# A hybrid decoder step on one core: the reciprocal square root of the norms as one GpSimd power

## The chip, the core and the metric

The kernel runs on one core of one Trainium2 chip. The metric is device time in microseconds (us) of the whole launch. A core has five engines with instruction queues of their own, which run in order and wait for each other by semaphores: TensorE (PE, with its weight loads PEld), VectorE (DVE), ScalarE (ACT), GpSimd (POOL) and SyncE (SP), which here issues nearly all DMAs.

## What is computed

The reference is one inference step of a 2-layer decoder, for a prompt of 2048 tokens and 8 samples of 8 tokens, with 1024 features. Each layer modulates its input, projects it (`z = h @ w_in[l]`), and gives pieces of z to four mixers that share the width: A differential attention, B a causal spatial gate, C a convolution module, D a gated linear recurrence (HGRN2). The outputs are gated, concatenated, projected, added to the residual and normalized. All of the norms need one number per row, or per row and head:

```
def _layer_norm(x, g, b):
    xc = xf - xf.mean(-1, keepdims=True)
    var = (xc * xc).mean(-1, keepdims=True)
    return xc * lax.rsqrt(var + EPS) * g + b
def _rms_norm(x, g):
    return xf * lax.rsqrt((xf * xf).mean(-1, keepdims=True) + EPS) * g
```

`_rms_norm` stands behind A and D (per head of 64 columns), `_layer_norm` in B and C (256 columns) and at the end of the layer (1024 columns).

## The kernel before

Tokens lie in tiles of 128 rows, 16 tiles for the prompt and one of 64 rows for the samples. A layer has two phases.

**Projections** (in the trace about 0 to 1040 us for layer 0 and 1640 to 2640 us for layer 1). In two groups of 1024 tokens, slabs of w_in are loaded, split by ACT and POOL into a high and a low part (`wh`, `wl`; the subtraction is `sub_lo`, L172, mostly on POOL), and multiplied on PE in three products into PSUM tiles `z`. The work of B, C and D is woven in: B's gate norm (`b_v`), C's 31 taps on DVE (`c_taps`, L1013) and its norm (`c_norm`), D's chain of blocks (`d_levels`) and its head norm (`d_norm`).

**Attention and output** (about 1040 to 1640 us and 2640 to 3202 us). For each block of query tiles and head, PE makes the scores (L668), DVE takes the row maximum from PSUM (L672), ACT the exponential (L676), DVE combines the two softmaxes (L697, L702), PE transposes (L715), ACT copies (L717), PE multiplies by the values (L720). The end of `attn_value` (from L731 on) sums squares per head, calls rsqrt for `sma` and scales `ot` by the result (L742); POOL applies the gain (L746). One block behind, `out_tile` does the output projection (L1360 to L1362), residual and LayerNorm of a tile; its rsqrt is that of `smo`, used by `nb` (L1372) and by ACT (L1376), after which POOL applies gain and offset (L1377, L1378).

`rsqrt(v, M, n, who, pool)` (L174 to L191) starts from the exponent bits (shift L179 on DVE, subtraction L181) and makes three Newton steps. With `pool` false it runs on DVE alone in 11 instructions (L179, L181, three times L183, L189, L190). With `pool` true, one shift stays on DVE and 13 instructions run on POOL (L181, three times L183, L185, L186, L187). There are 124 calls. The table KN sets who runs where: D (20 calls, up to 8 columns) and the sample's attention (2 calls, 4 columns) on POOL; A (40 calls, 4 or 2 columns), the LayerNorm of the outputs (34 calls, 1 column), B (18 calls, 2 columns or 1) and C (10 calls, 4 columns or 1) on DVE. The names of the columns carry the stream: `smd`, `sms`, `sma`, `smo`, `smb`, `smc`, with `y` for the result, `a` and `i` for the helpers.

The order of each engine's queue is not the order of the code: the tile framework simulates the program with its own durations and priorities and lays every queue out by that simulation. A change of one helper therefore moves instructions on all engines.

Of the kernel before, what the change touches and what calls it, by code (L numbers as in the profile page):

```python
# [9 lines left out]
F32 = mybir.dt.float32  # L10
F32R = mybir.dt.float32r
BF16 = mybir.dt.bfloat16
I32 = mybir.dt.int32
U8 = mybir.dt.uint8
AF = mybir.ActivationFunctionType
ALU = mybir.AluOpType
# [52 lines left out]
def hymba_step_kernel(  # L69
# [21 lines left out]
    # order, engines and buffers: P* offsets of priority, E* / L* / R* choice of engine, the others counts and orders  # L91
# [16 lines left out]
    def cpy(k, out, in_):  # L108
        """copy by ScalarE or VectorE"""
        (nc.vector.tensor_copy if KN[k] else nc.scalar.copy)(out, in_)  # L110
# [18 lines left out]
    # pools of the phase: PSUM banks of the projections, a second bank for transposes  # L129
# [21 lines left out]
    def st(tag, dt=F32):  # L151
        """rows of 512 of the streams that run beside each other: zs slabs, ms branches, os input and output"""
        return stp.tile([P, 512], dt, tag=tag, name=nm(tag), bufs=NST[tag])

    # small columns: width by stream
# [18 lines left out]
    def rsqrt(v, M, n, who, pool=True):  # L174
        """1 / sqrt(v) in place for v [M, n] > 0: estimate from the exponent bits, three Newton steps."""
        i = sm(who, "i", 2)[0:M, 0:n]
        y = sm(who, "y", 2)[0:M, 0:n]
        a = sm(who, "a", 2)[0:M, 0:n]
        nc.vector.tensor_scalar(i, v.bitcast(I32), 1, None, op0=ALU.logical_shift_right)  # L179
        eng = nc.gpsimd if pool else nc.vector  # L180
        eng.tensor_scalar(y.bitcast(I32), i, -1.0, float(0x5F3759DF), op0=ALU.mult, op1=ALU.add)  # L181
        for _ in range(3):
            eng.tensor_tensor(a, v, y, ALU.mult)  # L183
            if pool:
                eng.tensor_tensor(a, a, y, ALU.mult)  # L185
                eng.tensor_scalar(a, a, -0.5, 1.5, op0=ALU.mult, op1=ALU.add)  # L186
                eng.tensor_tensor(y, y, a, ALU.mult)  # L187
            else:
                eng.scalar_tensor_tensor(a, a, -0.5, y, op0=ALU.mult, op1=ALU.mult)  # L189
                eng.scalar_tensor_tensor(y, a, 1.5, y, op0=ALU.add, op1=ALU.mult)  # L190
        return y  # L191

    def gate2(dst, t, x):
        """2 silu(x) = (tanh(x / 2) + 1) x, given t = tanh(x / 2)"""
        nc.vector.scalar_tensor_tensor(dst, t, 1.0, x, op0=ALU.add, op1=ALU.mult)  # L195

# [7 lines left out]
    nc.vector.tensor_copy(identb, ident)  # L204
    cmaskb = cp.tile([P, 128], BF16, name="cmaskb")
# [7 lines left out]
    # page indices: row = (layer * NPOOL + page) * 128 + partition  # L213
# [15 lines left out]
    # conditioning vectors, transposed  # L229
# [50 lines left out]
    def mod(l, Lx, part, mp, bank=None):  # L280
        """shift, 1 + scale or gate of the rows of c, features on partitions."""
        dst = (Lx.shT, Lx.sc1T, Lx.gT)[part]
        for half in range(2):
# [7 lines left out]
            # the four sums are added once features are on partitions  # L291
# [23 lines left out]
    def prep(l, Lx, hp):  # L315
        """small tensors of a layer; hp: those that only the first phase needs"""
# [19 lines left out]
        with tc.tile_pool(name=nm("prep"), reuse_waits="tile", bufs=1) as pp:  # L336
# [16 lines left out]
            # lower bound: cumulative softmax over the layers, without the first  # L353
# [18 lines left out]
            # head norms; A and D carry the 1/2 of their gate  # L372
# [4 lines left out]
            # lambda of the differential attention  # L377
# [11 lines left out]
            # convolution taps  # L389
# [7 lines left out]
            # 1/4: the halves of the swish and of the gate  # L397
# [3 lines left out]
            # spatial weights, lower triangle  # L401
# [10 lines left out]
            # 1/2 of the gate in the weights and in the bias  # L412
# [13 lines left out]
    # state kept between the groups of a layer  # L426
# [92 lines left out]
    def tok_pairs(g):  # L519
        """(first token column, global tile, number of tiles, rows, is sample)"""  # L520
        out = [(i * P, g * GT + i, 2, P, False) for i in range(0, GT, 2)]
        if g == 0:
            out.append((TG, NT, 1, NS, True))
        return out
# [19 lines left out]
    def mix(main, n, *fills):  # L544
        """main (about n steps) with each fill (generator, steps, share of main over which it is spread) in between"""
# [18 lines left out]
    # ================= A: differential attention =================  # L564
# [55 lines left out]
    def attention(l, t0, nt, Lx, ap, act=None):  # L620
        """nt tiles of queries from tile t0"""
# [31 lines left out]
    def attn_probs(qi, qt, kst, l1, Lx, ap):  # L653
        """p1 - lam (l1 / l2) p2, unnormalized; l1"""
# [6 lines left out]
        for m in range(2):  # L661
            pms = []
            for pc, n in enumerate(sizes):
# [7 lines left out]
                # negated running maximum  # L671
# [7 lines left out]
            if npc > 1:  # L679
                # factor of the first part, whose maximum may have been smaller  # L680
# [24 lines left out]
    def attn_value(qi, pm, vst, acc, ls, j4, nt, hd, act, Lx, l, ap):  # L705
        """values of even key tiles on the lower columns of the array, of odd ones on the upper"""
# [21 lines left out]
        # transposed, the two halves of the columns added  # L728
# [11 lines left out]
        ss = rsqrt(ss, P, nt, "a", KN["RA"] and act is None)  # L740
# [8 lines left out]
    def attention_sample(l, Lx, Sx, ap):  # L749
# [91 lines left out]
        ss = rsqrt(ss, NS, 4, "s", KN["RS"])  # L841
# [6 lines left out]
    # ================= gates =================  # L848
# [12 lines left out]
    def gate_pair(l, g, h, ca, cb):  # L861
        """two slabs, by block of tokens: the first block is done with early"""
# [29 lines left out]
    # ================= B: spatial gate =================  # L892
    def b_v(l, g, h, Lx):
        def consume(ps, ti, n, M, smpl):
# [9 lines left out]
            rstd = rsqrt(rstd, M, n, "b", KN["RB"])  # L904
# [32 lines left out]
    # ================= C: convolution =================  # L937
# [81 lines left out]
    def c_norm_(l, g, C, acc, t0, n, smpl, Lx):  # L1019
# [13 lines left out]
            rstd = rsqrt(rstd, M, nt, "c", KN["RC"])  # L1033
# [24 lines left out]
    # ================= D: HGRN2 =================  # L1058
    def d_v(l, g, h, Sx, dp):
        Sx.di = dp.tile([P, GT, 256], F32, name=nm("di"))  # L1060
        if g == 0:
            # the sample rows on both halves of the partitions
# [12 lines left out]
    def d_init(g, Sx, dp):  # L1075
        """buffers of the chain of blocks, late ones first: they take the place of the convolution's"""
# [41 lines left out]
    def d_gate(f, p, n, Lx, Sx):  # L1118
        """f in place, and 1 - f"""
# [6 lines left out]
    def d_levels(q, f, k, n, levels, dp, Sx):  # L1126
        """masked products of all levels for blocks of 64 tokens: source tokens of a pair of blocks on partitions,
        (head, pair, target token) along the row (sample: the two heads on the partition halves); the products of a
        block with the one before it are left in PSUM; leaves prefix and suffix products."""
# [7 lines left out]
        def product(s, col, A, ia, B, ib, hh, par):  # L1137
            # the row tiles of the two heads work at the same time: never in one quadrant of a bank
# [49 lines left out]
    def d_norm(po, M, nq, dst, Lx):  # L1188
        """RMS norm over the 64 value columns of each head; po: [M, nq*64] in PSUM"""
# [5 lines left out]
        ss = rsqrt(ss, M, nq, "d", KN["RD"])  # L1195
# [4 lines left out]
    def d_block(l, g, p, b, q, f, Lx, Sx, dp):  # L1200
        k = d_gate(f, p, 512, Lx, Sx)
        att, sx, E = yield from d_levels(q, f, k, 512, LEVELS + (64,), dp, Sx)
        # source tokens of a pair of blocks x target tokens; the target before the source stays zero
# [78 lines left out]
    # ================= output projection, residual, LayerNorm =================  # L1282
    def out_weights(l, op):
        """w_out in two parts, and the rows of the epilogue"""
# [16 lines left out]
    def out_gate(l, O, smpl):  # L1301
        """gate rows of the sample or of the prompt"""
# [7 lines left out]
    # order of the rows of w_out: A and D (transposed here), B and C (features on partitions already)  # L1310
# [251 lines left out]
```

## Time and profile before

| what | value |
|---|---|
| time, median of 3 runs | 3179.31 us (3175.09 to 3195.48) |
| profiled execution: span | 3202.3 us, 22.99 us above the median of the runs |
| PE, DVE, ACT, POOL busy | 2881.2, 2280.8, 1223.5, 1122.6 us |
| granted TensorE clock, mean | 0.954 |

The span runs from the first to the last instruction of one profiled execution; that execution has no other time of its own in the data, so its span stands for it. A busy time is the time in which the engine had an instruction in work, a wait inside an instruction included. Matmuls overlap, and their ends are modelled.

### The profile page before, as it was taken

How to read it: one execution, taken by the hardware profiler on the slowest of the kernel's cores; microseconds unless marked ns; L12 is line 12 of the kernel's file. 1: busy time of each engine (PE TensorE's matmuls, PEld its weight loads, DVE VectorE, ACT ScalarE, POOL GpSimd, SP SyncE). 2: the span in 40 equal slices, each digit the busy share in tenths (PEclk: the TensorE clock that was granted, in tenths of full speed). 3: DMA queues.
4: the chain of work that ended last, by engine and by line, in shares of the span. 5: the costliest groups of instructions: out<-in, count | busy, mean ns of one | idle time of the engine just before them, and what ended most of it. 6: DMA issues, size and time to landing. Idle time of an engine off the chain costs nothing. (4 is left out here: it accounts for less than half of the span.)

```text
span 3202.3 us, 56179 instructions
## 1 busy us (share of the span) xinstructions
PE 2881.2 (90%) x20888; PEld 2260.0 (71%) x20888; DVE 2280.8 (71%) x5280; ACT 1223.5 (38%) x2564; POOL 1122.6 (35%) x1173
## 2 busy tenths in 40 slices
PE   6998999898999889979879989998989888997997
PEld 4888876688864466657668878776888656765665
DVE  3666883377692599988866667833776938998897
ACT  3111223312211466676642112233122137667663
POOL 4334455333230323412343443554342431241232
PEclk9999999899999899989989999998999998998998
DMA  6122323223324754546441222232232254544652
GB/s 224 61 72 85 90 83 119 79 64 93 111 90 154 192 148 129 142 103 162 122 149 57 74 88 87 86 120 81 64 105 88 69 152 120 132 130 110 150 154 72
DMA packets 343747, 353.26 MB, mean 110 GB/s; under 512 B 59728, under 2 KB 249718, under 8 KB 343459
## 3 DMA queue, kind: packets, MB, share of 16 engines
q1 hardware_dynamic: 337330, 332.90, 36.6%
q0 software_dynamic: 6144, 16.79, 1.8%
q8 instruction: 165, 2.70, 0.4%
q14 instruction: 108, 0.88, 0.1%
HBM read 266.44 MB, written 83.33 MB: 109 GB/s over the span
## 5 line engine op out<-in xcount | busy, mean ns | idle before, releaser
L515 PE MATMUL z<-hh,wh 128*128 128x512 f32 (+1 forms) x1440 | 526.5, 366 | 20.9 <-DVE zs L195 19.1
L172 POOL TENSOR_TENSOR wl<-raw,wh 128x512 fp32r<-128x512 f32 x224 | 323.1, 1455 | 609.1 <-ACT wh L110 562.8
L517 PE MATMUL z<-hh,wl 128*128 128x512 f32 (+1 forms) x1440 | 520.1, 362 | 0.0
L516 PE MATMUL z<-hl,wh 128*128 128x512 f32 (+1 forms) x1440 | 519.0, 361 | 0.0
L506 PE MATMUL z<-wh,hh 128*128 128x256 f32 (+1 forms) x1360 | 399.2, 294 | 12.6 <-issue 4.4
L1013 DVE SCALAR_TENSOR_TENSOR acc<-glu,cw,acc 128x512 f32<-128x512 f32 x480 | 402.2, 885 | 3.2
L507 PE MATMUL z<-wl,hh 128*128 128x256 f32 (+1 forms) x1360 | 394.8, 290 | 5.9 <-issue 5.9
L676 ACT ACTIVATE P<-S,stt 128x1024 f32<-128x1024 f32 (+7 forms) x384 | 332.9, 868 | 174.3 <-DVE stt L672 124.6
L508 PE MATMUL z<-wh,hl 128*128 128x256 f32 (+1 forms) x1360 | 395.7, 291 | 3.8 <-issue 3.6
L672 DVE TENSOR_REDUCE stt<-S 128x1 f32<-128x1024 f32 (+7 forms) x384 | 344.7, 905 | 62.1 <-PE S L670 45.1
L515 PEld LDWEIGHTS z<-hh,wh 128*128 128x128 f32 x1440 | 274.1, 190 | 81.7 <-DVE zs L195 23.5
L517 PEld LDWEIGHTS z<-hh,wl 128*128 128x128 f32 x1440 | 273.9, 190 | 50.9 <-issue 12.2
L516 PEld LDWEIGHTS z<-hl,wh 128*128 128x128 f32 x1440 | 274.0, 190 | 49.5 <-issue 13.8
L110 ACT CAST wh<-raw 128x512 fp32r<-128x512 f32 x224 | 133.8, 619 | 420.4 <-DMA raw<-in_w_in_dram 279.3
L668 PE MATMUL S<-K,Q 128*128 128x512 f32 (+3 forms) x640 | 226.8, 429 | 64.2 <-ACT P L676 53.6
L506 PEld LDWEIGHTS z<-wh,hh 128*128 128x128 f32 (+1 forms) x1360 | 262.0, 193 | 23.5 <-issue 10.0
L507 PEld LDWEIGHTS z<-wl,hh 128*128 128x128 f32 (+1 forms) x1360 | 261.8, 193 | 9.3 <-issue 7.8
L508 PEld LDWEIGHTS z<-wh,hl 128*128 128x128 f32 (+1 forms) x1360 | 261.9, 193 | 7.5 <-issue 5.2
L1360 PE MATMUL z<-woh,zs 128*128 128x512 f32 (+1 forms) x480 | 200.4, 417 | 16.1 <-ACT zs L110 10.1
L715 PE MATMUL T<-cst,P 128*128 128x128 f32 x1088 | 189.6, 303 | 25.1 <-DVE P L697 19.6
L172 POOL TENSOR_TENSOR zs<-os,zs 128x512 fp32r<-128x512 f32 (+1 forms) x64 | 84.3, 1319 | 348.0 <-ACT zs L110 339.1
L720 PE MATMUL X<-ph,V 128*64 128x128 f32 x2176 | 198.3, 296 | 8.1 <-ACT ph L717 7.6
(374 smaller groups left out, 5649.0 us busy)
## 6 DMA issues: line engine op xcount, KB each, us to landing
raw<-in_w_in_dram SPq DMA_DIRECT2D x128, 256.0 KB
K<-kh SPq DMA_DIRECT2D x224, 128.0 KB
K<-kl SPq DMA_DIRECT2D x224, 128.0 KB
mw<-in_w_ada_dram SPq DMA_DIRECT2D x96, 256.0 KB
raw<-in_w_in_dram SPq DMA_DIRECT2D x192, 128.0 KB
os<-gat SPq DMA_DIRECT2D x64, 256.0 KB
gat<-zs SPq DMA_DIRECT2D x48, 256.0 KB
os<-in_x_prompt_dram SPq DMA_DIRECT2D x32, 256.0 KB
```

Of the source, the lines that this page charges most:

```text
L172: eng.tensor_tensor(out, x, hi.bitcast(F32), ALU.subtract)
L506: nc.tensor.matmul(ps, hh[:, k, tok:tok + M], wh[:, k, :], start=(k == 0), stop=False)
L507: nc.tensor.matmul(ps, hh[:, k, tok:tok + M], wl[:, k, :], start=False, stop=False)
L508: nc.tensor.matmul(ps, hl[:, k, tok:tok + M], wh[:, k, :], start=False, stop=(k == KT - 1))
L515: nc.tensor.matmul(ps, wh[:, k, ms], hh[:, k, c0:c0 + n], start=(k == 0), stop=False)
L516: nc.tensor.matmul(ps, wh[:, k, ms], hl[:, k, c0:c0 + n], start=False, stop=False)
L517: nc.tensor.matmul(ps, wl[:, k, ms], hh[:, k, c0:c0 + n], start=False, stop=(k == KT - 1))
L668: nc.tensor.matmul(s[:, o:o + w], qt[:, m, :], kst[pc * 2 + o // 512][:, m, 0:w], start=True, stop=not diag)
L672: nc.vector.tensor_reduce(col(m, pc), s[:, :n], AX.X, ALU.max, negate=True)
L676: nc.scalar.activation(p[:, :n], s[:, :n], AF.Exp, bias=col(m, pc), scale=1.0, accum_out=l1 if m == 0 and npc == 1 else col(m, 2 + pc))
L1013: nc.vector.scalar_tensor_tensor(av, src(j), Lx.cw[:, c, j:j + 1], av, op0=ALU.mult, op1=ALU.add)
L1360: nc.tensor.matmul(po[0:M], a, wh[:, k, :], start=(i == 0), stop=False)
```

## The change

`rsqrt` keeps its name and loses the argument that chose the engine. It now is a single POOL instruction, v to the power of a constant column tile that holds -0.5, set once by a memset. All 124 calls take this form. Elsewhere only comments go. Lines behind the new constant stand 11 lower than before (L1372 is L1361 now, L672 is L661).

```
     cmaskb, identb ...
+    mhalf = cp.tile([P, 8], F32, name="mhalf")
+    nc.gpsimd.memset(mhalf, -0.5)
...
-    def rsqrt(v, M, n, who, pool=True):
-        """1 / sqrt(v) in place for v [M, n] > 0: estimate from the exponent bits, three Newton steps."""
-        i = sm(who, "i", 2)[0:M, 0:n]
+    def rsqrt(v, M, n, who):
+
         y = sm(who, "y", 2)[0:M, 0:n]
-        a = sm(who, "a", 2)[0:M, 0:n]
-        nc.vector.tensor_scalar(i, v.bitcast(I32), 1, None, op0=ALU.logical_shift_right)
-        eng = nc.gpsimd if pool else nc.vector
-        eng.tensor_scalar(y.bitcast(I32), i, -1.0, float(0x5F3759DF), op0=ALU.mult, op1=ALU.add)
-        for _ in range(3):
-            eng.tensor_tensor(a, v, y, ALU.mult)
-            if pool:
-                eng.tensor_tensor(a, a, y, ALU.mult)
-                eng.tensor_scalar(a, a, -0.5, 1.5, op0=ALU.mult, op1=ALU.add)
-                eng.tensor_tensor(y, y, a, ALU.mult)
-            else:
-                eng.scalar_tensor_tensor(a, a, -0.5, y, op0=ALU.mult, op1=ALU.mult)
-                eng.scalar_tensor_tensor(y, a, 1.5, y, op0=ALU.add, op1=ALU.mult)
+        nc.gpsimd.tensor_tensor(y, v, mhalf[0:M, 0:n], ALU.pow)
         return y
...
-        ss = rsqrt(ss, P, nt, "a", KN["RA"] and act is None)
+        ss = rsqrt(ss, P, nt, "a")
```

The other five calls (streams s, b, c, d, o) lose their last argument in the same way. Counted over the whole program, DVE goes from 5282 to 4138 instructions and POOL from 1178 to 1017; PE (17222), ACT (2166) and SP (1856) keep theirs.

The first place is DVE's queue in the attention of layer 0, around the LayerNorm of the second prompt tile (`smo_12228` before, `smo_11777` now). Before:

```order
L181 TENSOR_SCALAR smoy_12232<-smoi_12231 128x1
L692 TENSOR_TENSOR stt_12509<-stt_12509 128x1
L702 SCALAR_TENSOR_TENSOR P_12521<-P_12536,stt_12509,P_12521 128x128
L183 TENSOR_TENSOR smoa_12233<-smo_12228,smoy_12232 128x1
L189 SCALAR_TENSOR_TENSOR smoa_12233<-smoa_12233,smoy_12232 128x1
L190 SCALAR_TENSOR_TENSOR smoy_12232<-smoa_12233,smoy_12232 128x1
L683 SCALAR_TENSOR_TENSOR ls_12508<-stt_12547 128x1
L183 TENSOR_TENSOR smoa_12233<-smo_12228,smoy_12232 128x1
L189 SCALAR_TENSOR_TENSOR smoa_12233<-smoa_12233,smoy_12232 128x1
L190 SCALAR_TENSOR_TENSOR smoy_12232<-smoa_12233,smoy_12232 128x1
```

Now, at the same place, from the variance to the use of its reciprocal root:

```order
L1357 BN_AGGR omv_11775<-obs_11712 128x2
L1331 TENSOR_TENSOR os_11794<-z_11798,os_11791 128x512
L1359 TENSOR_SCALAR smo_11777<-omv_11775 128x1
L661 TENSOR_REDUCE stt_12060<-S_12061 128x1
L672 SCALAR_TENSOR_TENSOR stt_12022<-stt_12022 128x1
L1361 SCALAR_TENSOR_TENSOR smo_11778<-omv_11775,smoy_11780 128x1
L661 TENSOR_REDUCE stt_12060<-S_12067 128x1
```

The eleven steps are gone from DVE's queue, and two instructions of the attention stand between the variance and the use of its root (L1361). Over all calls of the two phases the median number of instructions that stand there is 2 for `smo` and 3 for `sma`.

The second place is POOL's queue at that time:

```order
L1325 TENSOR_TENSOR os_11705<-os_11704,os_11702 128x512
L1367 TENSOR_TENSOR x_11640<-x_11640,lnb_10715 128x512
L172 TENSOR_TENSOR zs_11707<-os_11705,zs_11706 128x512
L177 TENSOR_TENSOR smay_11424<-sma_11419,mhalf 128x4
L735 TENSOR_TENSOR ms_11426<-ms_11426,ag_385 128x256
L177 TENSOR_TENSOR smoy_11780<-smo_11777,mhalf 128x1
L172 TENSOR_TENSOR zs_11796<-os_11794,zs_11795 128x512
L1325 TENSOR_TENSOR os_11809<-os_11808,os_11806 128x512
```

The powers (L177) stand in one queue with the subtractions, gains and products of the output tiles; 22 of the 74 for `sma` and `smo` have a subtraction `zs` (L172), which needs ACT's copy first, right ahead of them. Before, none of the steps for `sma` and `smo` was in this queue.

The third place is POOL's queue at the first head norm of D in layer 0. Before, from the product ahead of it to the gain behind it:

```order
L580 TENSOR_TENSOR zs_1404<-zs_1404,zs_1405 128x16x16
L181 TENSOR_SCALAR smdy_2258<-smdi_2257 128x8
L183 TENSOR_TENSOR smda_2259<-smd_2254,smdy_2258 128x8
L185 TENSOR_TENSOR smda_2259<-smda_2259,smdy_2258 128x8
L186 TENSOR_SCALAR smda_2259<-smda_2259 128x8
L187 TENSOR_TENSOR smdy_2258<-smdy_2258,smda_2259 128x8
```

Now:

```order
L569 TENSOR_TENSOR zs_1338<-zs_1338,zs_1339 128x16x16
L177 TENSOR_TENSOR smdy_2259<-smd_2256,mhalf 128x8
L568 TENSOR_TENSOR zs_1406<-zs_1406,zs_1407 128x16x16
L569 TENSOR_TENSOR zs_1406<-zs_1406,zs_1407 128x16x16
L1187 TENSOR_TENSOR ms_2253<-ms_2253,dgn_386 128x512
```

Of the 13 steps (the four rows L183 to L187 stood three times) one is left, and it has moved ahead of two products of the rotary embedding.

## Rows read from the trace of the kernel before

**Rows 1.** The page: busy time, share of the span, instructions of each engine.

```profile
PE 2881.2 (90%) x20888; PEld 2260.0 (71%) x20888; DVE 2280.8 (71%) x5280; ACT 1223.5 (38%) x2564; POOL 1122.6 (35%) x1173
```

**Rows 2.** Windows: from:to, length, busy us (instructions) by engine, clock, DMA.

```profile
core 0: us, PE busy (x) PEld busy (x) DVE busy (x) ACT busy (x) POOL busy (x), PEclk, DMA share, GB/s
0.00:1040.00 1040.00, 950.57 (x7378) 762.16 (x7378) 639.13 (x1396) 242.91 (x492) 380.31 (x448) 0.97 0.33 102
1040.00:1640.00 600.00, 523.76 (x3172) 372.70 (x3171) 505.56 (x1253) 372.98 (x800) 183.92 (x149) 0.93 0.54 142
1140.00:1380.00 240.00, 216.66 (x1384) 157.90 (x1385) 228.47 (x549) 159.78 (x343) 85.68 (x68) 0.98 0.48 127
1640.00:2640.00 1000.00, 918.42 (x7319) 772.65 (x7317) 646.35 (x1395) 254.06 (x517) 401.61 (x455) 0.97 0.31 92
2640.00:3202.00 562.00, 488.46 (x3023) 352.50 (x3023) 489.75 (x1238) 353.58 (x757) 156.76 (x122) 0.93 0.48 125
```

**Rows 3.** Waits from 1100 to 1600 us, ACT and DVE: total us, times, longest.

```profile
ACT P L676 <- DVE stt L672: 65.7, 42, 5.6
DVE stt L672 <- PE S L670: 18.3, 22, 2.4
```

**Rows 4.** Windows of DVE's instructions on tiles smaa, smai, smoa, smoi, in turn.

```profile
1040.00:3202.00 2162.00, 84.02 (x360) 0.95 0.42 114
1140.00:1380.00 240.00, 22.04 (x72) 0.98 0.48 127
...
1040.00:3202.00 2162.00, 22.92 (x80) 0.95 0.42 114
1140.00:1380.00 240.00, 6.28 (x16) 0.98 0.48 127
...
1040.00:3202.00 2162.00, 73.22 (x306) 0.95 0.42 114
1140.00:1380.00 240.00, 18.56 (x74) 0.98 0.48 127
...
1040.00:3202.00 2162.00, 9.95 (x68) 0.95 0.42 114
1140.00:1380.00 240.00, 2.30 (x16) 0.98 0.48 127
```

**Rows 5.** Timeline (start, duration) of the last rsqrt, which nothing disturbs.

```profile
3193.42 0.15 DVE L179 TENSOR_SCALAR smoi<-smo 128x1 int32<-128x1 int32 x1
...
3195.55 0.16 DVE L1372 SCALAR_TENSOR_TENSOR smo<-omv,smoy 128x1 f32<-128x1 f32 x1
```

**Rows 6.** Timeline of a Newton step of A beside a subtraction on POOL.

```profile
1112.97 1.23 DVE L183 TENSOR_TENSOR smaa<-sma,smay 128x4 f32<-128x4 f32 x1
...
1112.73 1.45 POOL L172 TENSOR_TENSOR wol<-raw,woh 128x512 fp32r<-128x512 f32 x1 [1.02 <-ACT woh L1293]
```

**Rows 7.** Groups on POOL by form: count, busy us, mean ns.

```profile
L183 POOL TENSOR_TENSOR smda<-smd,smdy 128x8 f32<-128x8 f32 x48 | 10.6, 222 | 3.8
L172 POOL TENSOR_TENSOR wl<-raw,wh 128x512 fp32r<-128x512 f32 x224 | 323.1, 1455 | 609.1 <-ACT wh L110 562.8 <-PE S L1140 26.5 <-issue 11.0
```

**Rows 8.** Timeline of one head norm of D: first and last Newton step, its use.

```profile
153.09 0.20 POOL L181 TENSOR_SCALAR smdy<-smdi 128x8 int32<-128x8 int32 x1
...
157.20 0.20 POOL L187 TENSOR_TENSOR smdy<-smdy,smda 128x8 f32<-128x8 f32 x1
157.59 0.68 DVE L1197 TENSOR_TENSOR ms<-T,smdy 128x512 f32<-128x512 f32 x1
158.34 1.40 POOL L1198 TENSOR_TENSOR ms<-ms,dgn 128x512 f32<-128x512 f32 x1 [0.94 <-DVE ms L1197]
```

**Rows 9.** Waits of POOL from 1040 to 1640 us.

```profile
POOL zs L172 <- ACT zs L110: 214.6, 27, 86.8
POOL ms L746 <- DVE ms L742: 97.0, 11, 41.9
POOL x L1377 <- ACT x L1376: 96.8, 14, 16.9
```

**Rows 10.** The group of D's use of its root on DVE, by form.

```profile
L1197 DVE TENSOR_TENSOR ms<-T,smdy 128x512 f32<-128x512 f32 x16 | 11.0, 685 | 10.5 <-POOL smdy L187 10.4
```

More of the change, by code (lines that the diff above doesn't have):

```diff
@@ L840, in attention_sample @@
         nc.vector.tensor_scalar(ss, ss, 1.0 / 64.0, EPS, op0=ALU.mult, op1=ALU.add)
-        ss = rsqrt(ss, NS, 4, "s", KN["RS"])
+        ss = rsqrt(ss, NS, 4, "s")
         on = st("ms")
@@ L903, in consume @@
             nc.vector.tensor_scalar(rstd, mv[0:M, 0:n, 1], EPS, None, op0=ALU.add)
-            rstd = rsqrt(rstd, M, n, "b", KN["RB"])
+            rstd = rsqrt(rstd, M, n, "b")
             nb = sm("b")[0:M, 0:n]
@@ L1032, in c_norm_ @@
             nc.vector.tensor_scalar(rstd, mv[0:M, 0:nt, 1], EPS, None, op0=ALU.add)
-            rstd = rsqrt(rstd, M, nt, "c", KN["RC"])
+            rstd = rsqrt(rstd, M, nt, "c")
             nc.vector.scalar_tensor_tensor(nb, mv[0:M, 0:nt, 0], -1.0, rstd, op0=ALU.mult, op1=ALU.mult)
@@ L1194, in d_norm @@
         nc.vector.tensor_scalar(ss, ss, 1.0 / 64.0, 4.0 * EPS, op0=ALU.mult, op1=ALU.add)
-        ss = rsqrt(ss, M, nq, "d", KN["RD"])
+        ss = rsqrt(ss, M, nq, "d")
         d3 = dst.rearrange("p (a v) -> p a v", v=64)
@@ L1370, in out_tile @@
         nc.vector.tensor_scalar(rstd, mv[0:M, 1:2], EPS, None, op0=ALU.add)
-        rstd = rsqrt(rstd, M, 1, "o", KN["RO"] and not last)
+        rstd = rsqrt(rstd, M, 1, "o")
         nc.vector.scalar_tensor_tensor(nb, mv[0:M, 0:1], -1.0, rstd, op0=ALU.mult, op1=ALU.mult)
```

## The prediction

> **What bounds the kernel now.** I read the page's busy times first: PE is busy for 90% of the span, DVE for 71%, POOL for 35% [rows 1]. The average hides two regimes, so the windows come next [rows 2]. In the two projection phases (0 to 1040 and 1640 to 2640 us) PE is busy 950.57 of 1040 and 918.42 of 1000 us and DVE only 639.13 and 646.35: PE bounds. In the two attention phases DVE nearly draws level with PE (505.56 to 523.76, and 489.75 to 488.46), and in the steady stretch from 1140 to 1380 us DVE is busy 228.47 of 240 us, 95%, against 216.66 for PE and 159.78 for ACT [rows 2]. The waits of the phase point the same way: ACT's exponentials stood 65.7 us for DVE's row maximum, while DVE's maximum stood 18.3 us for PE [rows 3]. So DVE is the engine that sets the pace of attention, and work taken from it there can shorten the span; work taken from it elsewhere is mostly hidden behind PE.
>
> **What leaves DVE in attention.** The streams a and o (40 and 34 calls) are called there alone. Their 11 steps a call are the four pairs of rows of DVE's helper tiles: 84.02 + 22.92 + 73.22 + 9.95 = 190.1 us in 814 instructions, which is 74 calls of 11 [rows 4]; a call costs 2.57 us. In the steady stretch it is 22.04 + 6.28 + 18.56 + 2.30 = 49.2 of DVE's 228.47 us [rows 2, 4]. An undisturbed call lasts 3195.55 - 3193.42 = 2.13 us [rows 5], so 74 x 2.13 = 158 us are work and 32 us are stalls inside the steps. Such a stall is seen where a step of 1.23 us began while POOL's subtraction ran (1112.73 to 1114.18) and ended with it at 1114.20; the undisturbed step is 0.16 [rows 5, 6].
>
> The Trainium skill (SBUF — State Buffer, section Who interferes with whom) says that a VectorE instruction with two SBUF inputs and a GpSimd instruction that reads SBUF exclude each other, the later one waiting for the whole of the earlier one. The trace agrees in the pair just named. By that rule the 32 us belong to POOL's instructions, and a neighbour with two inputs would inherit them: the relief would be 158 us and the sum below 3118 us. I keep 190, since the commonest neighbour, the row maximum, reads PSUM.
>
> **The price of the power.** No row shows one. It cannot well be shorter than POOL's shortest arithmetic on so few columns, 0.20 us, and as one instruction for the same function it should not be longer than the 13-step chain it replaces on POOL, 153.09 to 157.40, 4.3 us [rows 8]. Between them I scale: POOL's step costs 0.222 us on 8 columns and 1.455 on 512, hence 2.45 ns a column [rows 7]; thirteen passes over 4 columns in one instruction are 0.222 + 13 x 4 x 0.00245 = 0.35 us, over 8 columns 0.48. I take 0.4 us for all, an estimate, nearer to the low end because a fixed cost is paid once instead of 13 times.
>
> The Trainium skill (GPSIMD Engine Reference, section Instruction dispatch) prices the first call of a freshly loaded GpSimd kernel at about 6 us. Nothing in the trace of before shows it; by it the sum would be 6 us longer, once.
>
> **The new wait.** What used to follow inside DVE's queue now goes to POOL and back. A hop is 0.07 us (DVE's L1197 ends at 158.27, POOL's L1198 starts at 158.34 [rows 8]), so the round trip is 0.07 + 0.4 + 0.07 = 0.54 us. The new order puts a median of 2 (o) or 3 (a) other DVE instructions between variance and use; at 505.56 / 1253 = 0.40 us each [rows 2] that covers 0.8 or 1.2 us. With POOL free, the trip is hidden. POOL is busy 183.92 of 600 us there [rows 2] with instructions of up to 1.45 us [rows 6], so on average 0.31 x 0.7 = 0.2 us come on top. If the use comes too early, DVE stops, and behind it the next row maximum, ACT's exponential and PE's scores. The new order rests on durations that are not the chip's, so I charge 0.6 us a call: 74 x 0.6 = 44 us.
>
> **How much of it reaches the span.** Net relief of DVE is 190 - 44 = 146 us. In the steady stretch DVE would need 228.47 - 49.2 = 179 us, and PE, busy 216.66, is next: taken as stiff, it lets 240 us shrink by 23.3, which is 0.47 of the 49.2. PE's busy time would give way, as part of it is the modelled tail of lone matmuls; against that, every hand-over in the loop DVE, ACT, PE has a latency. I take 0.47 for the whole: 146 x 0.47 = 69 us.
>
> **The rest.** D's head norm: POOL's chain of 4.3 us shrinks to one instruction, DVE stood 10.4 us for its end in 16 calls [rows 8, 10], and POOL loses 12 instructions a call ahead of the slab subtractions. Most of POOL's work there is hidden behind PE; I count 8 us. B and C (28 calls): DVE loses 2.13 us a call and gains a round trip in a queue shared with slab subtractions of 1.455 us [rows 7]; PE covers both, so nothing (+30 us if the cover fails, -15 if a PSUM tile comes free earlier each time). The sample's two calls, the memset and the removed shifts: nothing, there are too few. DMAs: the count on SP and POOL is as before. Every queue is laid out anew, though; I give that no sign, and 10 us either way.
>
> **Sum.** 3202.3 - 69 - 8 = 3125 us for the profiled execution. Its span is 22.99 us above the median of the runs, so I scale by 3179.31 / 3202.3 = 0.9928: **3103 us**, 2.4% less.
>
> **The rivals.**
> - *All of DVE's relief lands.* PE's busy time turns out elastic, and DVE stays the bound: 146 + 8 = 154 us, so 3048 and scaled 3026 us. For it speaks that ACT waits for DVE and PE for ACT; against it, PE's 216.66 of 240 us [rows 2].
> - *The waits eat the gain.* POOL's queue often stands still: from 1040 to 1640 us it stood 214.6 us (27 times, 7.9 us each) at `zs` for ACT and 96.8 us (14 times) at `x` [rows 9], together 52% of the time. A power that lands behind such a head at random waits half of some 7.5 us: 0.52 x 3.7 = 1.9 us, with the 0.6 above 2.5 us a call, 185 us in all, as much as was removed. Then only D's 8 us and a few more remain: 3189, scaled 3166 us. That the new order puts powers where the old order's spare time was speaks against it; that 22 of 74 stand right behind a `zs` speaks for it.
> - *Slower: DVE is held by POOL's queue.* The place is the use of the root, L742 and L1372 (L731 and L1361 now), on DVE. The point from which it decides is 2.57 us of wait a call, the price removed. If every power stands behind half of such a halt, DVE waits 3.7 + 0.54 - 1.0 of cover = 3.2 us, 74 x 3.2 = 240 us against 190, +50; B and C, where PE's PSUM tiles wait for DVE, add the 30 above: 3282, scaled 3259 us. The power at its upper end of 4.3 us has the same effect, (4.3 + 0.14 - 1.0) x 74 = 255 us, +65: 3267, scaled 3244 us.
> - *The change does not do what it says.* The instruction lists exclude that: 1144 fewer on DVE, 161 fewer on POOL. What they leave open is that the relaid queues matter more than the roots; that case lies in the second rival.
>
> **The numbers.** My forecast 0.50 (its own range 3065 to 3145), all lands 0.13, eaten 0.20, slower 0.17. Less than 1% (32 us) cannot be told from no change. Faster: 0.50 + 0.13 + 0.02 of the eaten case = 0.65; same 0.18; slower 0.17. The range runs from 3030, which leaves out about half of the first rival, to 3205, which takes in the second and leaves out most of the slower case: together about 0.2 outside.
>
> **What would show it.** Right: the attention phases together shorter by some 70 us, projections by less than 15; DVE's busy time in attention down by 170 to 190 us; a power of 0.3 to 0.5 us; DVE's waits for POOL's `smay` and `smoy` under 50 us in all; PE busy above 92% of the steady stretch. Wrong: a power above 1.5 us, waits for the roots above 150 us, or attention no shorter although DVE has fallen to 75%, which would mean that PE or the hand-overs bounded it all along. A span that changes mainly in the projections would show that the relaid queues decided.

## The result, and the profile after

| kernel | median, us | runs, us |
|---|---|---|
| before | 3181.18 | 3175.09 to 3195.48 (4) |
| changed | 3222.75 | 3206.13 to 3229.73 (4) |

The changed kernel is slower: its ratio to before is 1.0109 (95% interval 1.0082 to 1.0135), where 3103 us, 0.975, was forecast. The two profiles don't show that directly: the profiled span of before lay 21 us above the median of its runs, that of the changed kernel belongs to the fastest of its runs, 3206.13 us. Their spans, 3202.3 and 3203.8 us, are therefore no comparison of the two kernels; places within them are.

The page of the changed kernel, busy times by engine, as in [rows 1]:

```profile
PE 2886.2 (90%) x20888; PEld 2256.9 (70%) x20888; DVE 2146.3 (67%) x4136; ACT 1226.4 (38%) x2564; POOL 1162.8 (36%) x1012
```

The windows of [rows 2], same columns (the last one ends at 3203 us, with this span):

```profile
0.00:1040.00 1040.00, 959.86 (x7408) 764.16 (x7408) 618.95 (x1233) 246.14 (x495) 374.13 (x331) 0.97 0.34 103
1040.00:1640.00 600.00, 514.75 (x3096) 364.45 (x3095) 460.67 (x839) 369.41 (x789) 208.91 (x178) 0.92 0.49 136
1140.00:1380.00 240.00, 210.07 (x1308) 155.00 (x1307) 198.40 (x348) 150.66 (x322) 85.25 (x73) 0.95 0.43 119
1640.00:2640.00 1000.00, 923.86 (x7342) 774.99 (x7342) 627.23 (x1228) 256.03 (x518) 395.27 (x345) 0.97 0.31 94
2640.00:3203.00 563.00, 487.75 (x3048) 353.25 (x3046) 439.41 (x838) 354.77 (x762) 184.47 (x159) 0.94 0.45 126
```

From 1140 to 1380 us DVE fell from 228.47 to 198.40 us, 95% to 83%. If DVE had set the pace and nothing else had changed, PE would have done more matmuls in these 240 us; it did fewer, 1308 where it had done 1384. DVE got free time, and nothing moved up into it.

The waits of [rows 3], from 1100 to 1600 us (total us, times, longest):

```profile
ACT P L665 <- DVE stt L661: 57.2, 42, 5.0
DVE stt L661 <- PE S L659: 28.4, 27, 3.6
```

ACT waits less for the maximum and DVE more for the scores. (DVE waits at a second line of the scores too, L668 before and L657 now; with it the sums are 24.8 and 44.9 us, where the prediction read 18.3 for before.) DVE's waits for roots, over the whole span:

```profile
DVE smb L895 <- POOL smby L177: 23.6, 16, 3.5
...
DVE ms L731 <- POOL smay L177: 8.4, 11, 2.3
DVE ms L1186 <- POOL smdy L177: 8.1, 8, 1.8
DVE smo L1361 <- POOL smoy L177: 7.1, 9, 1.9
```

DVE stands 15.5 us for the 74 roots of the attention, where 44 had been charged; the round trip is not what the kernel loses. What the power itself takes, by form (count, busy us, mean ns):

```profile
L177 POOL TENSOR_TENSOR smay<-sma,mhalf 128x4 f32<-128x4 f32 x24 | 27.9, 1163 | 162.0 <-DVE sma L728 115.9 <-DVE stt L676 28.7 <-DVE smo L1359 16.6
L177 POOL TENSOR_TENSOR smdy<-smd,mhalf 128x8 f32<-128x8 f32 x16 | 27.3, 1708 | 71.6 <-DVE smd L1183 71.6
L177 POOL TENSOR_TENSOR smoy<-smo,mhalf 128x1 f32<-128x1 f32 x32 | 20.4, 639 | 95.3 <-DVE smo L1359 77.9 <-DVE stt L663 9.3 <-DVE stt L681 7.0
...
L177 POOL TENSOR_TENSOR smay<-sma,mhalf 128x2 f32<-128x2 f32 x16 | 11.3, 706 | 69.4 <-DVE sma L728 58.9 <-DMA K<-kl 9.1 <-DVE smo L1361 1.1
```

0.64, 0.71, 1.16 and 1.71 us for 1, 2, 4 and 8 columns: 1.6 to 4.3 times the 0.4 us of the prediction. The first power of the run starts at 152.26 us and takes 1.68 us, so the extra 6 us for a first call, which the prediction mentions, don't show in it.

### The profile page after: what moved, and what is told of

Read it like the earlier page. It is cut to its first block, busy times and chain, and to the rows that moved or that the text cites. A ratio compares the mean times of both kernels' runs of the same rounds, so it can differ in the third digit from the quotient of the medians.

```text
span 3203.8 us, 54892 instructions
## 1 busy us (share of the span) xinstructions
PE 2886.2 (90%) x20888; PEld 2256.9 (70%) x20888; DVE 2146.3 (67%) x4136; ACT 1226.4 (38%) x2564; POOL 1162.8 (36%) x1012
## 5 line engine op out<-in xcount | busy, mean ns | idle before, releaser
L504 PE MATMUL z<-hh,wh 128*128 128x512 f32 (+1 forms) x1440 | 527.2, 366 | 23.8 <-DVE zs L182 21.1
L172 POOL TENSOR_TENSOR wl<-raw,wh 128x512 fp32r<-128x512 f32 x224 | 312.1, 1406 | 520.6 <-ACT wh L110 437.0
L661 DVE TENSOR_REDUCE stt<-S 128x1 f32<-128x1024 f32 (+7 forms) x384 | 344.0, 905 | 94.7 <-PE S L659 63.2
L657 PE MATMUL S<-K,Q 128*128 128x512 f32 (+3 forms) x640 | 226.5, 428 | 71.1 <-ACT P L665 55.9
L1349 PE MATMUL z<-woh,zs 128*128 128x512 f32 (+1 forms) x480 | 203.6, 424 | 21.8 <-ACT zs L110 15.7
L706 ACT COPY ph<-T 128x512 f32<-128x512 f32 (+2 forms) x320 | 162.3, 523 | 137.0 <-PE T L704 135.2
L1351 PE MATMUL z<-woh,zs 128*128 128x512 f32 (+1 forms) x480 | 199.8, 416 | 12.9 <-POOL zs L172 12.6
```

Of the source, the lines that this page charges most:

```text
L172: eng.tensor_tensor(out, x, hi.bitcast(F32), ALU.subtract)
L504: nc.tensor.matmul(ps, wh[:, k, ms], hh[:, k, c0:c0 + n], start=(k == 0), stop=False)
L657: nc.tensor.matmul(s[:, o:o + w], qt[:, m, :], kst[pc * 2 + o // 512][:, m, 0:w], start=True, stop=not diag)
L661: nc.vector.tensor_reduce(col(m, pc), s[:, :n], AX.X, ALU.max, negate=True)
```

## The experiments

Two things changed at once: the roots, and the order of every queue. To part them, most kernels below are laid out in one way and then edited: instructions are taken out of the finished queues or put in, nothing is laid out again, and each wait is set anew to the work it stood for. "Old order" is the layout of the kernel before, "new order" that of the changed one; a layout here is the order of all queues together with the buffers and waits that came with it, and these were not parted. All ratios are to the kernel before, run on the same chip in the same turn, in brackets the 95% interval.

### Roots and order apart

**The old order without the Newton steps.**

```
 L179, L181           the bare estimate stays (less exact roots; the time is what is asked for)
-L183, L189, L190     three times in each of the 74 calls: 666 instructions out of DVE's queue
```

> Every queue in the order of the kernel before; the three Newton steps of the 74 roots of the attention (streams a and o) are left out, 666 instructions or about 155 us of VectorE's 190, and the roots are then the bare estimates. No GpSimd power, no new wait, no new order. The forecast's theory (VectorE's work bounds attention, 0.47 of what leaves it reaches the span): 0.47 x 155 = 73 us shorter, about 3108. Rival (VectorE was not the bound; PE with the hand-overs of scores, maxima and exponentials sets the pace): 0 to 15 us shorter, 3166 to 3181.

Measured 0.9891 [0.9871, 0.9912], 35 us shorter. VectorE's work does bound attention in part: half of the 73 us that the forecast's share gives, and more than the 15 us that the rival allowed.

**The old order with the powers of the attention.**

```
-L179 ... L190        all 11 steps of the 74 calls, out of DVE's queue
+TENSOR_TENSOR smay<-sma,mhalf (pow)   into POOL's queue, where L179 stood in the laid-out program
```

> Every queue in the order of the kernel before; the 74 chains of the attention on VectorE are replaced by one GpSimd power each, put in GpSimd's queue where the chain's first step stood in the simulated order. The other 50 roots stay as before. Forecast's theory: about 69 us shorter, 3112. Rival 'the new order of the queues is what costs': no slower than before, 3165 to 3185. Rival 'the trip to GpSimd and back is what costs, whatever the order': slower, 3205 to 3230.

Measured 0.9837 [0.9818, 0.9855]: 52 us shorter than before. The change to the roots of the attention does what it was forecast to do, at three quarters of the size.

**The new order with the chains, and with the bare estimate.** Both leave the changed kernel's other 50 powers.

```
-TENSOR_TENSOR smay<-sma,mhalf (pow)   74 of them, out of POOL's queue
+L179, L181, 3 x (L183, L189, L190)    into DVE's queue, one behind the other   (newton_new)
+L179, L181                            alone                                    (lean_new)
```

> Every queue in the order of the changed kernel; its 74 powers of the attention are replaced by the 11-step chain on VectorE, put where the power stood in the simulated order. The other 50 roots stay powers. Forecast's theory (VectorE's work bounds): 0.47 x 190 = 89 us above the changed kernel, about 3310. Rival 'the order costs': like the changed kernel, 3215 to 3240. Rival 'the trip to GpSimd costs': back to 3175 to 3195.

> Every queue in the order of the changed kernel; its 74 powers of the attention are replaced by the two steps of the bare estimate on VectorE, so neither the Newton work nor the trip to GpSimd is there. The other 50 roots stay powers. Rival 'the order costs': still slower than before, 3205 to 3225. Rival 'the trip to GpSimd costs': 3140 to 3185. Forecast's theory: at most what the cheap chain leaves, about 3110.

Measured 1.0536 [1.0515, 1.0556] and 1.0101 [1.0074, 1.0128]. With neither the Newton work nor a trip to POOL in its attention, the new order is as slow as the changed kernel (1.0109). So it is not the attention's powers. It is not the editing either: this kernel is edited too, and no faster. With the chains the new order is 4.2% slower than with the powers (1.0536 against 1.0109), where the old order differs by 1.6%. The chains stand in one piece there, each step waiting for the last. In the trace of newton_new DVE has nothing but their steps at work for 165 us, and stands another 26 us ahead of them; in the old order (same_order, counted in attention) it has nothing but chains at work for 124 us. That this is the whole reason is not shown.

**All 124 powers in the old order** (pow_old_all): as pow_old, for all streams.

> Every queue in the order of the kernel before; all 124 chains are replaced by one power each at the chain's place: the whole change without the new order. Theory 'the new order costs, the powers gain': at least as fast as with the 74 powers of the attention alone (ratio 0.984 to before), 0.978 to 0.985, 3113 to 3136 us, since D, B and C are covered by TensorE. Rival 'the powers of the projections cost, by blocking GpSimd's queue ahead of the slab subtractions': slower than those 74 alone, 0.990 or more.

Measured 0.9881 [0.9860, 0.9902]. This is the whole change without the new order, and it would have been 1.2% faster. The powers of the projections cost something, against the first theory, and less than the rival said. Where, DVE's waits for roots in this run say (the lines of before):

```profile
DVE smc L1034 <- POOL smcy L179: 20.5, 5, 8.5
DVE smb L906 <- POOL smby L179: 12.4, 9, 2.3
DVE ms L742 <- POOL smay L179: 2.5, 3, 0.9
DVE smo L1372 <- POOL smoy L179: 1.7, 3, 0.7
```

B and C wait 33 us for POOL, A and the output tiles 4.2 us. Without B and C (pow_old_aods):

> Every queue in the order of the kernel before; the roots of the attention, of D's head norm and of the samples (96 calls) are powers, the 28 of B and C stay chains on VectorE. With the attention's 74 alone the ratio to before was 0.984, with all 124 0.988. Theory 'B's and C's trips to GpSimd cost, D gains': 0.978 to 0.983. Rival 'D's powers cost': 0.986 to 0.990, as with all 124.

Measured 0.9842 [0.9817, 0.9867]: B's and C's 28 powers cost about 0.4%, some 12 us (the intervals of the two runs just overlap). D's 20 gain nothing that can be seen: DVE's wait for D's roots, 11.4 us in pow_old, is gone in this run, and no time with it.

**The same instructions laid out by the framework** (pow_ao): the 74 powers of the attention in the code, the other 50 roots as before.

```
+        if who in "ao":
+            nc.gpsimd.tensor_tensor(y, v, mhalf[0:M, 0:n], ALU.pow); return y
```

> The 74 roots of the attention as powers and the other 50 as before, laid out anew by the framework: the same instructions as in the run with the 74 powers in the old order (ratio 0.984), only their order is another. Theory 'the new order costs': 1.000 to 1.015, as the whole change. Rival 'it was the order that the powers of the projections brought': 0.980 to 0.990.

Measured 1.0066 [1.0044, 1.0088], against 0.9837 for the same instructions in the old order. By this pair a new layout costs 1.0066 / 0.9837 = 1.023, by the pair of the whole change, whose layout is another, 1.0109 / 0.9881 = 1.023: 2.3%, 73 us.

### What a comparison can see, and small moves

same_order is the kernel before with an unused constant (+ one memset on POOL); nudge_old and nudge_new put `nc.vector.memset(y, 1.0)` ahead of each root of the attention, in before and in the changed kernel; new_patt sets PATT=20 for PATT=0 in the changed kernel's table.

> The kernel before with the constant tile and its memset, read by nothing: TensorE's, VectorE's, ScalarE's and SyncE's queues are unchanged, GpSimd's has one memset more and two neighbours swapped at its start. Every theory: 0.998 to 1.002; what it differs by is what the comparison can't see.

> The kernel before with one memset of the result column on VectorE ahead of each of the 74 roots of the attention, laid out anew with them: 74 short instructions, about 74 x 0.1 = 7 us of VectorE, and otherwise only another order. Theory 'any new order costs, because the old one was the good one': 1.005 or more. Rival 'orders near the old one are as good': 1.000 to 1.004.

> The changed kernel with one memset of the result column on VectorE ahead of each of the 74 roots of the attention, laid out anew with them. Rival 'the new order is one bad draw among many': well off the changed kernel's 1.011, either way, say 0.985 to 1.000. Theory 'what the framework makes of attention without the chains on VectorE is systematically worse': 1.006 to 1.016.

> The changed kernel with one number of its table of priorities another (attention's own work 20 places earlier), laid out anew with it; the work is the changed kernel's. Rival 'one bad draw': 0.985 to 1.003. Theory 'systematically worse without the chains': 1.005 to 1.020, since no single number gives the old order back.

Measured 0.9985 [0.9966, 1.0005], 1.0001 [0.9986, 1.0015], 1.0110 [1.0088, 1.0132] and 1.0045 [1.0029, 1.0062]. The two layouts are not fragile: 74 small instructions more leave the good one good and the bad one bad. One number of the table takes back 0.6%; so ranking the work otherwise gives part of the loss back.

### Which chain, and how much of it, the layout needs

```
 est_relaid   -for _ in range(3): (Newton)   in all 124 calls, laid out anew
 steps2, 1    range(3) -> range(2), range(1) in the 74 calls of a and o, laid out anew
 pow_a, pow_o if who in "a" / "o": power     the rest as before, laid out anew
```

> All 124 roots cut to the bare estimate (shift and subtraction on the engines of before, no Newton steps), laid out anew: no power, no trip, VectorE has some 190 us less work in all than before. The attention's part of it gave 0.989 in the old order. Theory 'laying out anew without the chains costs about 2%': 1.002 to 1.015. Rival 'only the powers' places make a bad order': 0.980 to 0.990.

> The 40 roots of the attention's heads (stream a) as powers, the other 84 as before, laid out anew. In the old order it should gain 40/74 of 1.6%, 0.991. Theory 'a's chain held the good order': 1.000 to 1.012. Rival 'o's chain held it': 0.988 to 0.996.

> The 34 roots of the output tiles (stream o) as powers, the other 90 as before, laid out anew. In the old order it should gain 34/74 of 1.6%, 0.9925. Theory 'a's chain held the good order': 0.990 to 0.996. Rival 'o's chain held it': 1.000 to 1.012.

> The chains of the 74 roots of the attention with two Newton steps instead of three, laid out anew: 222 instructions or some 52 us less on VectorE, no power. In the old order 0.9964 by the run without steps (0.989 for three). Theory 'the less work the layout sees on VectorE, the worse its order', in proportion: 1.003. Rival 'it turns at one point or by chance': 0.994 to 0.998 here or above 1.006.

> The same with one Newton step: 444 instructions or some 104 us less on VectorE. In the old order 0.9927. Theory 'in proportion': 1.006. Rival 'it turns at one point or by chance': the same as with two steps, or back below 0.996.

| laid out with | measured | in the old order, measured or in proportion | order costs |
|---|---|---|---|
| est_relaid, no steps | 1.0094 [1.0073, 1.0116] | 0.989 (lean_old, attention alone) | 2.0% |
| steps1 | 1.0028 [1.0011, 1.0045] | 0.9927 | 1.0% |
| steps2 | 0.9947 [0.9929, 0.9965] | 0.9964 | -0.2% |
| pow_a | 0.9990 [0.9974, 1.0006] | 0.991 | 0.8% |
| pow_o | 1.0089 [1.0070, 1.0108] | 0.9925 | 1.6% |

Without any power the order gets worse as the chain gets shorter, and either stream's power brings a worse one, that of the output tiles more so. One step of three may go at no cost. The last two keep the executed instructions (those of pow_old) and change only the chain that the layout saw:

```
 range(3) -> range(2) or range(4) for a and o, laid out; then each chain out, one power in
```

> Laid out with two Newton steps in each root of the attention, then each of these 74 chains replaced by one GpSimd power; the other 50 roots as before. Theory 'the more VectorE work the layout sees, the better its order': between 0.984 (laid out with three steps) and 1.007 (laid out with the power), since the run with two steps itself kept a good order, nearer to the first: 0.984 to 0.990. Rival 'chance': anywhere from 0.975 to 1.007.

> The same, laid out with four Newton steps. Theory 'the more VectorE work the layout sees, the better its order': 0.975 to 0.984. Rival 'the order of three steps is the best because the table of priorities was chosen on it', or chance: 0.987 or more.

Measured 0.9845 [0.9819, 0.9871] and 0.9970 [0.9957, 0.9983]. Laid out with a power, two, three and four steps, the same instructions run at 1.0066, 0.9845, 0.9837 and 0.9970. So "the more work the layout sees on VectorE, the better" is wrong above three steps, and what makes a layout good stays open. A range of 2.3% between layouts of one program is what the runs show.

### Where the new order loses

The attention phases, cut in each trace from the first row maximum to the last normalization of an output tile on ACT (windows, columns as in [rows 2]; layer 0, layer 1). The old order with the chains (same_order):

```profile
1054.20:1644.60 590.40, 515.53 (x3175) 373.58 (x3173) 517.60 (x1287) 380.16 (x821) 194.32 (x156) 0.93 0.53 147
2592.40:3164.40 572.00, 496.86 (x3080) 356.18 (x3080) 493.82 (x1252) 359.56 (x772) 157.46 (x125) 0.95 0.46 126
```

The old order with the 74 powers (pow_old):

```profile
1053.50:1628.10 574.60, 512.37 (x3173) 373.43 (x3172) 462.32 (x880) 379.59 (x821) 226.77 (x192) 0.92 0.55 151
2568.10:3118.80 550.70, 495.80 (x3080) 358.27 (x3080) 440.91 (x845) 359.78 (x772) 191.27 (x162) 0.94 0.47 131
```

The old order with all powers (pow_old_all):

```profile
1069.90:1641.80 571.90, 511.52 (x3173) 372.96 (x3172) 462.69 (x880) 379.23 (x821) 227.90 (x192) 0.93 0.55 151
2593.50:3142.30 548.80, 491.91 (x3080) 354.36 (x3080) 440.01 (x846) 359.76 (x772) 190.32 (x161) 0.95 0.47 131
```

The changed kernel, which has the same instructions in the new order:

```profile
1064.80:1677.20 612.40, 522.89 (x3141) 377.41 (x3139) 476.68 (x878) 377.94 (x812) 225.00 (x191) 0.91 0.51 140
2626.50:3198.70 572.20, 499.93 (x3080) 359.06 (x3080) 440.74 (x845) 358.87 (x772) 187.08 (x162) 0.94 0.46 127
```

Both layers together: 1162.4 us with the chains, 1125.3 with the attention's powers, 1120.7 with all, 1184.6 in the new order.

The executions of the last two differ by 56.5 us in span (3147.3 and 3203.8), their attention by 63.9: in this pair the new order loses in attention, and nowhere else. In pow_ao attention takes 1189.0 us, 63.7 more than in pow_old, of 81.2 us in span; there some of the difference, or of the luck of two executions, lies outside. How far such a sum moves by itself can be seen from nudge_old, whose median is that of before: 1180.1 us in its profile, 18 more than in same_order. So a difference of under 20 us between two such sums tells nothing.

The work there is nearly the same (32 matmuls fewer in the window of layer 0): DVE is busy 902.70 and 917.42 us, ACT 738.99 and 736.81, PE 1003.43 and 1022.82, part of it at a lower granted clock (0.91 for 0.93 in layer 0). The rest is idle time: PE stands 44.5 us more, DVE 49.2, ACT 66.1. They don't stand together. The time in which PE, DVE and ACT are all idle at once, counted in the two traces over both layers, is 5.1 us in the old order and 5.9 in the new; PE and DVE are both idle for 21.1 and 22.2 us. The engines work more in turn and less side by side.

Who stands for whom in layer 0, in the old order (pow_old_all):

```profile
ACT P L676 <- DVE stt L672: 51.0, 40, 3.7
ACT ph L717 <- PE T L715: 50.6, 48, 3.7
...
PEld S L668 <- ACT P L676: 39.2, 45, 3.0
...
PE S L668 <- ACT P L676: 28.0, 28, 2.6
...
DVE stt L672 <- PE S L670: 31.1, 35, 3.0
...
DVE stt L672 <- PE S L668: 8.9, 14, 1.3
```

and in the new (the changed kernel):

```profile
ACT ph L706 <- PE T L704: 69.5, 64, 4.2
ACT P L665 <- DVE stt L661: 62.9, 49, 5.0
...
PEld S L657 <- ACT P L665: 48.7, 56, 3.8
...
PE S L657 <- ACT P L665: 31.9, 34, 3.7
...
DVE stt L661 <- PE S L659: 34.0, 35, 3.6
DVE stt L661 <- PE S L657: 16.5, 23, 2.5
```

Most hand-overs of the loop grew: maximum to exponential by 11.9 us, transpose to copy by 18.9, exponential to the next scores by 9.5 (PE's weight loads) and 3.9 (PE), scores to maximum by 2.9 and 7.6. In layer 1 the same six lines grew too, by 1.8 to 18.3 us. None of these lines is a root, and none is a single long stall (5.0 us at most). The smaller ones are within what these lines differ by between executions of the old order, and not all lines grew: in layer 0 PE and its weight loads wait 5.1 and 13.2 us for ACT's copy where they waited 5.5 and 14.2. Nor does a long wait alone make an order slow: in the kernel before, with the chains on DVE, the line from maximum to exponential is 71.9 us.

The line that parts the runs best is that from transpose to copy in layer 0: 48.1 to 53.2 us in the seven kernels that have the old order or that of nudge_old, 64.7 to 76.2 in the six that measured 1.0066 or more in another. It is no rule, since steps2 and pow_laid2 have 61.7 and 60.2 us and are fast.

No engine is busy throughout in the new order: the loop PE, DVE, ACT waits on itself, more often. The likely reason is that what used to stand between a hand-over and its use in each queue now stands elsewhere, but no run shows it. Which of the moved rows do it no run tells either; a hybrid of the two orders, one engine's queue from each, was not tried.

## Why the prediction was wrong

The step that failed is the last sentence of "The rest": "Every queue is laid out anew, though; I give that no sign, and 10 us either way." The new layout cost 2.3%, 73 us, which is more than the 69 us that attention was to gain. What in the new layout costs it stays open, beyond the fact that its engines stand for each other longer in attention. The last sign of the prediction pointed to the wrong place, too: that the relaid queues decide was to be seen in the projections, and it was seen in attention. The other steps, measured in the old order:

- *DVE sets the pace of attention*: right in part. With 814 instructions fewer on DVE, attention went from 1162.4 to 1125.3 us (37 us, twice the 18 us of nudge_old) while PE's busy time stayed (1012.39 to 1008.17). "Attention no shorter although DVE has fallen" did come true in the changed kernel, with DVE at 83% of the steady stretch, but the meaning given to it beforehand, that PE or the hand-overs had bounded it all along, was wrong: in pow_old less work on DVE makes attention shorter.
- *190.1 us leave DVE*: mis-sized. DVE's busy time in attention fell from 517.60 + 493.82 = 1011.42 to 903.23 us, by 108. The 190 us were the steps' own durations; part of that time another DVE instruction was at work too, and part passed to neighbours. Both can be counted. Without the steps' rows DVE's busy time in the trace of same_order is 887.1 us, 124.3 less, so some 60 of the steps' 187 us there lay beside other work on DVE. In the trace of before the same count gives 127.0 us, where the prediction had 190.1. Of the 124 us, 16 came back as longer neighbours: pow_old has 903.2 us, not 887.1. The largest growth is in the group of L683, a combination of single columns, in same_order (count, busy us, mean ns):

```profile
L683 DVE SCALAR_TENSOR_TENSOR ls<-stt 128x1 f32<-128x1 f32 x64 | 15.6, 244 | 1.0 <-ACT stt L681 1.0
```

  and in pow_old:

```profile
L683 DVE SCALAR_TENSOR_TENSOR ls<-stt 128x1 f32<-128x1 f32 x64 | 23.2, 363 | 3.7 <-ACT stt L681 3.6
```

  The view of that line gives its shortest, median and longest there, in ns:

```profile
L683 DVE SCALAR_TENSOR_TENSOR ls<-stt x64: 160/213/1275, 1196.3 to 3068.2; 128x1 f32<-128x1 f32 x64
```

  The same 64 instructions take 7.6 us more without the chains between them: 13 of them last over half a microsecond, where 2 did, and each of the 13 ends within 0.03 us of the end of a POOL instruction beside it, as the Newton step did [rows 6]. (Not every group grew; that of L692 fell by as much.) One of them in the timeline of pow_old:

```profile
1464.06 1.27 POOL L172 TENSOR_TENSOR zs<-os,zs 128x512 fp32r<-128x512 f32 x1 [4.94 <-ACT zs L110]
...
1464.18 1.15 DVE L683 SCALAR_TENSOR_TENSOR ls<-stt 128x1 f32<-128x1 f32 x1
```

  The rule of the Trainium skill (SBUF — State Buffer, section Who interferes with whom) is that a VectorE instruction with two SBUF inputs contends with a GpSimd instruction that reads SBUF. L683 reads two inputs and a scalar column, all in SBUF, and the trace agrees: 1.15 us in place of the usual 0.21 in the pair just shown. The prediction had worked out from it that such neighbours inherit the stalls, and had set that aside; they did inherit some, though the relief by that reckoning, 158 us, was still too high, as the larger part is the overlap.
- *The power takes 0.4 us*: 0.64 to 1.71 us, in attention up to 1.16. The sign of being wrong, above 1.5 us, was passed by D's 8 columns alone, and the longer power did no harm in attention: see the next point.
- *The new wait, 44 us*: 4.2 us in the old order, 15.5 in the new. What stands between variance and use was cover enough even for the longer power.
- *0.47 of the relief reaches the span*: of the 108 us that did leave, 37 us show in the attention windows (0.34), and 52 us in the medians (0.48), which also hold the projections. The sum, 69 us forecast and 52 measured, came out near in part by luck: the relief was put 82 us too high and the wait 40, and these two errors partly offset each other.
- *D 8 us, B and C nothing (+30 to -15)*: D nothing to be seen, B and C some 12 us slower, inside the bound.

Of the rivals, "DVE is held by POOL's queue" has the right sign and the wrong place: the waits for roots in the changed kernel's attention are 15.5 us, not the 240 that it needs. POOL's queue did change as it says: from 1040 to 1640 us its head now stands for the roots' inputs, as below, where `zs` alone took 214.6 us before [rows 9]; but lean_new, without these powers, is as slow. The last rival names the mechanism, "the relaid queues matter more than the roots", but files it under no gain.

```profile
POOL zs L172 <- ACT zs L110: 88.2, 12, 34.4
POOL smay L177 <- DVE sma L728: 85.2, 12, 17.1
...
POOL smoy L177 <- DVE smo L1359: 55.5, 7, 18.3
```

The version that beats both kernels is pow_old: the layout made with the chains, the attention's 74 roots then run as powers, the rest as before: 3130.25 us, 0.9837 of before (3183.39 us on the same chip). With D's powers as well (0.9842) or laid out with two steps (0.9845) it is the same within the intervals.

## What to carry to other kernels

Where a simulation lays out the queues, a local edit is two edits: price the new order with as much doubt as a layout of the same work has been seen to move the time (here 2.3%), and measure the edit in the old order before judging it. When an engine gets free time and its neighbours do less in the same stretch, look at the hand-overs of the loop line by line: if most of them grew a little and the engines stand in turn, suspect the order, and test it. The relief of an engine is read from what its total would lose, not from the durations of the instructions that go: strike their rows out of the trace of before and take its busy time again (here 127 us, where the durations add up to 190 and 108 were measured).

## What the runs showed of the hardware

- The power on POOL is priced by its columns: 0.64, 0.71, 1.16 and 1.71 us for 1, 2, 4 and 8 columns on 128 partitions, where POOL's ordinary step on 8 columns took 0.222 us [rows 7]. On 8 columns it still replaces a chain of 4.3 us [rows 8].
- TensorE's busy time is no constant of the work: for the same 3080 matmuls in the attention of layer 1 it was 491.91 us in pow_old_all, 499.93 in the changed kernel and 533.48 in newton_new. The mean granted clock there is 0.95, 0.94 and 0.87 of 2.4 GHz, a mean over stretches at 2.4 and at 1.2 GHz, and PE's busy share is 0.90, 0.87 and 0.82. The two windows of newton_new:

```profile
1070.40:1745.60 675.20, 548.54 (x3130) 390.82 (x3130) 546.55 (x1285) 377.95 (x812) 195.04 (x153) 0.86 0.47 127
2697.70:3348.80 651.10, 533.48 (x3080) 380.77 (x3080) 512.75 (x1252) 361.44 (x772) 159.87 (x125) 0.87 0.41 111
```

  In these three kernels the one whose PE stands more also has the lower clock and the slower matmuls, so part of what a bad order costs may be paid there. No run here shows that the one brings the other.
- An instruction on DVE with single columns in SBUF, 0.21 us as a rule (the median of L683), lasted up to 1.28 us in pow_old beside a POOL instruction that reads SBUF, and ended with it: 13 of 64 lasted over half a microsecond there, 2 of 64 in same_order.
